# Hybrid SSD and Conformer layer on one core: decay rows repeated by DMAs, step sizes folded into exponents, sums by matmuls, more convolution taps off VectorE, three units at the start

## The chip, the core and the metric

The kernel runs on one core of a Trainium2 chip. Its engines are TensorE (PE, with its weight loads as PEld), VectorE (DVE), ScalarE (ACT), GpSimd (POOL) and SyncE (SP), which here only issues DMAs. The metric is the time of one execution on the device in microseconds (us), as the median of several runs. Profiles come from one profiled execution each.

## The reference, cut to what matters

One layer of a diffusion backbone is applied to 512 latent tokens and 128 context tokens, with a width of 1024, all in float32. The change touches the first of its two sub-layers, token mixing:

```python
h = rms_norm(x, g_pre) * (1 + sc1) + sh1
proj = h @ w_in                       # z, x/B/C of the SSD, dt, and a, g of the Conformer branch
# (A) SSD, both directions, 16 heads, chunks of 128
dt = softplus(dt_raw + dt_bias);  a_cum = cumsum(dt * a)      # per chunk and head
decay[i, j] = exp(a_cum[i] - a_cum[j])  for i >= j, else 0
y_diag[i] = sum_j (C_i . B_j) * decay[i, j] * x[j] * dt[j]
y_off[i]  = (C_i . state before the chunk) * exp(a_cum[i])
y_ssd = rms_norm((y_fwd + y_bwd + x * d_skip) * silu(z))
# (B) Conformer branch
u = a * sigmoid(g);  u = depthwise conv over 31 taps(u);  u = silu(layer_norm(u))
x = x + g1 * rms_norm(concat(y_ssd, u) @ w_out)
```

The second sub-layer is a gated FFN of width 2816 with a 3x3 depthwise convolution between its up-projection and its gate. The final SSD states of the context tokens are outputs too.

## The kernel before

Data lie with channels on the 128 partitions and the 640 tokens (512 latent, then 128 context) along the free axis. A *unit* is one weight block, 128 x 1024 f32 (512 KB), giving 128 output channels. To keep float32 accuracy in the faster float32r matmuls, each weight and each activation is split in two parts: ACT copies it to float32r (`hi`, L165 for weights, L253 for activations), and POOL or DVE subtracts (`lo`, L167, L255). `mm3` (L261) forms hi x hi, hi x lo and lo x hi for each of 8 blocks of the contraction, in two column halves (384 and 256): 48 matmuls (L268) per unit. `fetch` (L133) loads units in order on SP's queue into two raw buffers (`wr`); there are three buffers each for `hi` and `lo`, and `get_unit` asks for two units ahead.

The framework orders each engine's instructions itself, by priority and an estimate of times when the program is built; each engine then runs its own list in order. `tc.issue_after(x)` puts an instruction behind `x` on its engine; `conv31` has a negative `high_priority`, so its taps fill what is left.

The stages up to the output projection:

- *Start.* x is loaded, its norm computed (column sums L326, square root L340, spread L334), and x multiplied by it (chunks 0 to 3 on DVE, L373; 4 to 7 on POOL, L375). In four steps `ada_first` (L290) produces the modulation of two chunks, DVE applies it (L385), and the first two units, g0 and a0, multiply those chunks.
- *`dtprep`* (L448). Small DVE and ACT operations give the step sizes `DT`, the cumulative decays `ACM`, the weights `WD` and `CDs`; the decays, split in two parts, are transposed into `acHL`.
- *Pairs of heads*, p = 0 to 7, in the order of the list `seq` (L181 to 211). Each pair projects xs, z, and g, a of a later pair. `ssd(p)` (L592): POOL makes x * dt (`xd`, L600); one-column selectors multiply `acHL` so that a head's decay row appears on all partitions in PSUM (L631); ACT takes Relu(ACM - row) per chunk (L637), then Exp (L645); DVE and POOL multiply by the masked products of C and B (L648); L666 multiplies with `xd`. `decays()` (L605) does the same for exp(a_cum), with a selector cast on DVE (L608) and matmuls L612. `ssd_tokens(p + 1)` transposes x and weights it (L559), `ssd_states(p + 1)` forms the chunk states (L573, L575), copies them (L577), stores the context states and runs the recurrence on POOL (L585, L588). The states enter by L655. `ssd_tail(p)` (L678) adds, multiplies by silu(z) and squares.
- *`conv31(p)`* (L707). 31 taps: the first on ACT (L718), then one DVE instruction per tap into PSUM (L721, L724, L725). `OFF[p]` taps (9 in all) go instead as ACT products (L730) and POOL additions (L734, L736). POOL adds the results to a running sum (L742).
- *LN and the "ahead" products.* `ln_stats` (L750) makes the mean and variance by column sums; `ahead_splits` (L844) splits the first five SSD outputs; `ahead_parts` (L851) multiplies them by their weights; `layer_norm` (L826) applies norm and Silu.

After that, the output projection starts at about 423 us of the profiled execution; the FFN follows and ends it.

## Time and profile before

| | |
|---|---|
| median of 3 runs | 1012.25 us (1012.11 to 1014.71) |
| profiled execution | 1010.71 us |
| its span | 1008.9 us |
| mean granted TensorE clock | 0.993 |
| data moved by DMA | 102.76 MB, mean 102 GB/s |

A profile page gives the busy time of each engine, its share of the span and its instructions; then the busy share of 40 slices, the DMA queues, the chain of waits that ended last, and groups of instructions by source line. In a group, "out<-in" names the tiles, "xN" counts, then come busy time and mean ns of one, and the idle time before them with what ended it. In the order of time each line has start, duration, engine, line, operation, tiles and count; a bracket holds the idle time before and what released it. Matmuls overlap in the pipeline, so the mean duration of one is longer than the distance between two.

### The profile page before, as it was taken

To read this page: it belongs to the slowest core of one execution; us is meant where nothing else is said; L and a number is where in the kernel's file an instruction comes from. 1 tells how busy PE (TensorE), PEld (TensorE's weight loads), DVE (VectorE), ACT (ScalarE), POOL (GpSimd) and SP (SyncE) were. 2 spreads that over 40 slices of the span, in tenths; PEclk is the share of its full clock that TensorE was granted. 3 is DMA by queue.
4 is the path that set the end of the run, shared out by engine and by line. 5 is a ranking of instruction groups with operands and counts; after the bars stand their busy time and mean duration, and the time that the engine had idled before them with its cause. 6 is when DMAs were issued, how large, how long until landed. Compare 5 with 4: busy or idle time off the path is not lost.

```text
span 1008.9 us, 18834 instructions
## 1 busy us (share of the span) xinstructions
PE 968.3 (96%) x7655; PEld 933.7 (93%) x7655; DVE 736.1 (73%) x1093; ACT 457.9 (45%) x766; POOL 588.8 (58%) x426
## 2 busy tenths in 40 slices
PE   4999999999999989999989999999999999999995
PEld 2789999999999978899979999999999999999995
DVE  3789999989999998672286798998988988400004
ACT  6244556674553856842364754233233236322211
POOL 2333877888887896443473696454454456543444
PEclk9999999999999999999999999999999999999998
DMA  9622121122212111559463422222222222222212
GB/s 345 229 80 79 53 94 63 54 74 64 74 43 66 41 50 41 167 165 391 156 206 106 147 84 64 85 70 77 85 71 76 84 70 68 79 79 74 79 37 105
DMA packets 42934, 102.76 MB, mean 102 GB/s; under 512 B 4832, under 2 KB 12768, under 8 KB 42848
## 3 DMA queue, kind: packets, MB, share of 16 engines
q1 hardware_dynamic: 42848, 101.56, 30.4%
q8 instruction: 60, 0.98, 0.4%
q14 instruction: 26, 0.21, 0.1%
HBM read 97.87 MB, written 3.67 MB: 101 GB/s over the span
## 4 chain that ended last, share of the span: by engine, by line
PE 81%; DVE 7%; ACT 5%; POOL 3%; issue 2%; DMA 2%; SPq 0%; POOLq 0%; ACTq 0%; DVEq 0%
PE ps L268 67%; PE ps L1112 3%; PE pq L268 2%; POOL wl L167 2%; PE pq L313 2%; PE pq L666 1%; DVE T L760 1%; ACT wh L165 1%; DVE ps L721 1%; PE pq L655 1%; PE pq L573 1%; DMA wr<-in_wout 1%; PE pq L294 1%; PE pq L631 1%; DMA T<-in_xT 1%
## 5 line engine op out<-in xcount | busy, mean ns | idle before, releaser
L167 POOL TENSOR_TENSOR wl<-wr,wh 128x1024 fp32r<-128x1024 f32 (+3 forms) x127 | 291.7, 2297 | 293.3 <-ACT wh L165 287.4
L268 PE MATMUL ps<-H,wh 128*128 128x384 f32 (+1 forms) x1636 | 322.1, 310 | 4.9 <-DVE M L421 2.2
L165 ACT ACTIVATE wh<-wr 128x1024 fp32r<-128x1024 f32 (+3 forms) x131 | 131.7, 1006 | 342.6 <-PE ps L268 196.8
L268 PE MATMUL ps<-T,wh 128*128 128x384 f32 (+1 forms) x1472 | 273.1, 306 | 1.9 <-ACT S L1080 1.9
L268 PEld LDWEIGHTS ps<-H,wh 128*128 128x128 f32 x1636 | 249.0, 188 | 9.1 <-issue 4.5
L1090 DVE SCALAR_TENSOR_TENSOR S<-ps,prms,S 128x441 f32<-128x441 f32 (+2 forms) x336 | 233.4, 695 | 29.7 <-ACT S L1080 19.2
L268 PEld LDWEIGHTS ps<-T,wh 128*128 128x128 f32 x1472 | 219.3, 188 | 2.3 <-ACT S L1080 2.2
L721 DVE SCALAR_TENSOR_TENSOR ps<-u,prms,ps 128x655 f32<-128x655 f32 x223 | 200.7, 900 | 9.9 <-ACT ps L718 5.4
L268 PE MATMUL ps<-H,wl 128*128 128x384 f32 (+1 forms) x818 | 194.8, 310 | 0.0
L268 PE MATMUL ps<-T,wl 128*128 128x384 f32 (+1 forms) x736 | 166.7, 306 | 0.0
L268 PEld LDWEIGHTS ps<-H,wl 128*128 128x128 f32 x818 | 128.8, 188 | 1.6 <-issue 1.2
L268 PEld LDWEIGHTS ps<-T,wl 128*128 128x128 f32 x736 | 113.0, 188 | 0.0
L341 DVE RECIPROCAL rsm<-rsm 128x160 f32<-128x160 f32 (+2 forms) x9 | 7.3, 815 | 141.5 <-ACT rsm L340 141.5
L268 PE MATMUL ps<-S,wh 128*128 128x384 f32 (+1 forms) x420 | 87.5, 312 | 1.7 <-DVE M L923 1.2
L268 PEld LDWEIGHTS ps<-S,wh 128*128 128x128 f32 x420 | 65.9, 188 | 4.3 <-issue 2.5
L268 PE MATMUL ps<-S,wl 128*128 128x384 f32 (+1 forms) x210 | 54.4, 308 | 0.3 <-POOL wl L167 0.3
L637 ACT ACTIVATE S<-pq,ACM 128x128 f32<-128x128 f32 x140 | 40.9, 372 | 18.3 <-PE pq L631 18.1
L1080 ACT ACTIVATE S<-ps,prms 128x640 f32<-128x640 f32 x42 | 36.5, 868 | 0.0
L268 PEld LDWEIGHTS ps<-S,wl 128*128 128x128 f32 x210 | 35.0, 188 | 0.5 <-POOL wl L167 0.5
L588 POOL TENSOR_TENSOR S<-S,stmp 128x128 f32<-128x128 f32 x36 | 18.6, 517 | 15.1 <-ACT S L577 11.2
L1193 POOL TENSOR_TENSOR H<-S,S 128x640 f32<-128x640 f32 x16 | 25.2, 1578 | 0.0
L648 POOL TENSOR_TENSOR S<-S,M 128x640 f32<-128x640 f32 x14 | 22.1, 1577 | 4.4 <-ACT S L645 4.4
(353 smaller groups left out, 1276.7 us busy)
## 6 DMA issues: line engine op xcount, KB each, us to landing
wr<-in_wup SPq DMA_DIRECT2D x44, 512.0 KB, 3.4
wr<-in_win SPq DMA_DIRECT2D x36, 512.0 KB, 3.5
T<-in_wada SPq DMA_DIRECT2D x49, 256.0 KB, 5.4
wr<-in_wdown SPq DMA_DIRECT2D x16, 512.0 KB, 3.4
wr<-in_wout SPq DMA_DIRECT2D x13, 512.0 KB, 3.4
H<-in_wada SPq DMA_DIRECT2D x23, 256.0 KB, 5.5
S<-in_wada SPq DMA_DIRECT2D x16, 256.0 KB, 5.9
wr<-in_wdown SPq DMA_DIRECT2D x8, 384.0 KB, 3.1
```

The costliest lines, as they stand in the source:

```text
L165: ac.activation(hi[:, :n], raw[:, :n], AF.Copy)
L167: lo_eng.tensor_tensor(lo[:, :n], raw[:, :n], hi[:, :n].bitcast(F32), SUB)
L268: last_mm[0] = te.matmul(out, w, x[:, c0:c1], start=first and i == 0, stop=last and i == 2)
L313: te.matmul(pt[32 * j:32 * j + 32, 0:P], cts[:, kc, :], w[:, j * P:(j + 1) * P], start=kc == 0, stop=kc == KD - 1, tile_position=(0, 32 * j))
L588: gp.tensor_tensor(now, now, tmp, ADD)
L637: ac.activation(r[:, c * P:(c + 1) * P], pb[:, (c - c0) * P:(c - c0 + 1) * P], AF.Relu, scale=-1.0, bias=ACM[:, c, row:row + 1])
L648: (ve if i % 2 or last else gp).tensor_tensor(r, r, cbm[g][d], MUL)
L721: ve.scalar_tensor_tensor(acc, u[:, j:j + UO], w(j), acc, MUL, ADD)
L1080: ac.activation(out, v, AF.Identity, bias=prm_col("ffn_b", i), scale=w(1, 1))
L1090: ve.scalar_tensor_tensor(ob, vl[:, r0 + a - 1:r1 + a - 1, q0 + b - 1:q1 + b - 1], w(a, b), ob, MUL, ADD)
L1112: te.matmul(pt[:, o:o + c1 - c0], w[k] if i in (1, 2) else w[:, k * P:(k + 1) * P], x[:, c0:c1], start=k == 0 and j == 0, stop=k == KD - 1 ...
L1193: gp.tensor_tensor(f_raw[q], a, b, MUL)
```

## The change

Decay rows: `dtprep` transposes `ACM` itself, stores it in a DRAM tile `acD` (32 rows, one for each head and direction, of 640), and `load_rows(p)` reads each row back onto all partitions by DMA. ACT's Relu and Exp then work in place on those tiles; the selectors and their matmuls are gone. `load_rows(p + 1)` is called after `ssd_tail(p)`, for the last pair at the statistics.

Step sizes: exp(a_i - a_j) * dt_j becomes exp of a sum with log(dt_j) in it. `AC2` is `ACM` less log(dt), shifted by `EB`, the largest log(dt) of a row, which is added back as the bias of Exp; so `xd` is not needed and L666 takes x itself.

Sums: `ln_stats` takes the column sums of all eight results instead of POOL's running sum. Taps: `OFF` grows from 9 to 30. Start: B0 is the third unit of the first loop; parameters come in two loads, `wdts` and `ids` later; DVE does all eight multiplications of x; the Sqrt table is loaded after the first Silu. A few orders on queues are fixed by `issue_after`.

```diff
-    sy.dma_start(prms, prm)
-    ids = sb.tile([P, 32], F32, tag="idhl", name="ids")
-    sy.dma_start(ids, idhl_d)
-    wdts = sb.tile([P, KD, 32], F32, tag="DTW", name="wdts")
-    sy.dma_start(wdts, wdt)
+    NEAR = _COLS["g_mix_pre"][1]
+    sy.dma_start(prms[:, 0:NEAR], prm[:, 0:NEAR])
...
-    FIRST = ("g0", "a0")
+    FIRST = ("g0", "a0", "B0")
...
-    s_proj("B0", "C0")
+    s_proj("C0")
...
-    ac.activation(cts, cts, AF.Silu)
-
-    ac.activation(sb.tile([P, 1], F32, tag="warm", name="warm"), epsc, AF.Sqrt)
+    cond = ac.activation(cts, cts, AF.Silu)
+
+    with tc.issue_after(cond.ins):
+        ac.activation(sb.tile([P, 1], F32, tag="warm", name="warm"), epsc, AF.Sqrt)
...
-    for s in range(1, 4):
+    firsts = [(get_unit(unit_of[n][0]), psum((0, 2)[i])) for i, n in enumerate(FIRST[:2])]
+    wdts = sb.tile([P, KD, 32], F32, tag="DTW", name="wdts")
+    sy.dma_start(wdts, wdt)
+    load_ada(1)
+    sy.dma_start(prms[:, NEAR:], prm[:, NEAR:])
+    ids = sb.tile([P, 32], F32, tag="idhl", name="ids")
+    sy.dma_start(ids, idhl_d)
+    for s in range(2, 4):
         load_ada(s)
     ada_first(0)
-    rs0 = slot("S12")
-    ac.activation(rs0, prs[:, 192:192 + T], AF.Copy)
     for k in range(KD):
-        if k < 4:
-            ve.tensor_tensor(xs_[k], xs_[k], prs[:, 192:192 + T], MUL)
-        else:
-            gp.tensor_tensor(xs_[k], xs_[k], rs0, MUL)
+        ve.tensor_tensor(xs_[k], xs_[k], prs[:, 192:192 + T], MUL)
+    firsts.append((get_unit(unit_of[FIRST[2]][0]), psum(1)))
...
-        ac.activation(aexp, prm_col("a_log", 0, 32), AF.Exp)
+        with tc.issue_after(hi_ins[0].ins):
+            ac.activation(aexp, prm_col("a_log", 0, 32), AF.Exp)
...
+        ve.tensor_scalar(by(a), DT, 1e-37, None, MAX)
+        ac.activation(n, a, AF.Ln)
+        ac.activation(w, n, AF.Exp, scale=-1.0)
+        ve.tensor_tensor(w, w, a, MUL)
+        ve.scalar_tensor_tensor(n, w, -1.0, n, ADD, ADD)
+        EB = sb.tile([P, 32], F32, tag="EB", name="EB")
+        ve.tensor_tensor(EB, by(n)[:, 0, :], by(n)[:, 1, :], MAX)
+        for c in range(2, NCH):
+            ve.tensor_tensor(EB, EB, by(n)[:, c, :], MAX)
+        AC2 = sb.tile([P, NCH, 32], F32, tag="AC2", name="AC2")
+        ve.tensor_tensor(AC2, ACM, by(n), SUB)
+        ve.tensor_tensor(AC2, AC2, EB.unsqueeze(1).to_broadcast([P, NCH, 32]), ADD)
...
+        acD = dr.tile([32, T], F32, tag="acD", name="acD")
+        sy.dma_start(acD, acT[0:32, :])
+
+    rows = {}
+
+    def load_rows(p):
+
+        last = p == NPAIR - 1
+        for h in range(2):
+            for d in range(2):
+                row = 2 * p + h + 16 * d
+                r = rows[p, h, d] = slot(f"{'H' if last else 'S'}{(12 if last else 6) + 2 * h + d}")
+                sy.dma_start(r, acD[row:row + 1, :].to_broadcast([P, T]))
+        for d in range(2):
+            e = rows[p, d] = slot(f"S{10 + d}")
+            for h in range(2):
+                row = 2 * p + h + 16 * d
+                sy.dma_start(e[64 * h:64 * h + 64, 0:L], acD[row:row + 1, 0:L].to_broadcast([64, L]))
...
-            ac.activation(t[:, 0:4 * P], pt, AF.Copy)
+            state_out[0] = ac.activation(t[:, 0:4 * P], pt, AF.Copy)
...
-        xd = []
-        for d in range(2):
-            o = slot(("M4", "H11")[d] if last else f"S{2 + d}")
-            a = 16 * d + 2 * p
-            gp.tensor_tensor(hq(o), hq(xt), DT[:, :, a:a + 2].unsqueeze(3).to_broadcast([P, NCH, 2, 64]), MUL)
-            xd.append(o)
...
             for d in range(2):
-                pea = psq(d)
-                te.matmul(pea[:, 0:L], sel[:, d].rearrange("p h q -> p (h q)"), acHL[:, 0:L], start=True, stop=True)
-                ea.append(slot(f"S{10 + d}"))
-                peas.append(pea)
-            for o, pea in zip(ea, peas):
-                ac.activation(o[:, 0:L], pea[:, 0:L], AF.Exp)
+                o = rows.pop((p, d))
+                ac.activation(o[:, 0:L], o[:, 0:L], AF.Exp)
+                ea.append(o)
...
+                r = rows.pop((p, h, d))
+                for c in range(NCH):
+                    rc = r[:, c * P:(c + 1) * P]
+                    if last and d:
+                        with tc.issue_after(z_done[0].ins):
+                            ve.tensor_scalar(rc, rc, AC2[:, c, row:row + 1], 0.0, SUB, MIN)
+                        continue
+                    ac.activation(rc, rc, AF.Relu, scale=-1.0, bias=AC2[:, c, row:row + 1])
...
-            ssd_exp[0] = ac.activation(r, r, AF.Exp, scale=1.0 if last and d else -1.0)
+            ssd_exp[0] = ac.activation(r, r, AF.Exp, scale=1.0 if last and d else -1.0,
+                                        bias=EB[:, 16 * d + 2 * p + h:16 * d + 2 * p + h + 1])
...
-                                  xd[d][:, c * P + 64 * h:c * P + 64 * h + 64],
+                                  xt[:, c * P + 64 * h:c * P + 64 * h + 64],
...
-    OFF = [1, 2, 1, 2, 1, 2, 0, 0]
+    OFF = [6, 6, 4, 4, 4, 4, 2, 0]
...
-        if p == 0:
-            usum[0] = slot("S17")
-            gp.tensor_copy(usum[0], o)
-        elif p < NPAIR - 1:
-            gp.tensor_tensor(usum[0], usum[0], o, ADD)
...
-        colsum(pm, 0, usum[0], 0, 160, True, False)
-        colsum(pm, 0, uc[NPAIR - 1], 0, 160, False, True)
+        for p in range(NPAIR):
+            colsum(pm, 0, uc[p], 0, 160, p == 0, p == NPAIR - 1)
...
+    bT[0] = slot("M2")
+    conv3_silu(firsts[2][1], 8, bT[0])
     dtprep()
...
             ssd_tail(it[1])
+            if it[1] + 2 < NPAIR:
+                load_rows(it[1] + 1)
         elif it[0] == "stats":
+            load_rows(NPAIR - 1)
...
             hi, lo = slot(f"H{k}", F32R), slot(LOSLOT[k], F32R)
-            ac.activation(hi, tp[k], AF.Copy)
+            with tc.issue_after(state_out[0].ins):
+                ac.activation(hi, tp[k], AF.Copy)
```

## The prediction

> **What bounds the kernel now.** I read the page first (shares, chain), then cut the span into windows by stage, then the groups, and last the order of time where a term of the sum stands. The page:

> ```profile
> span 1008.9 us, 18834 instructions
> PE 968.3 (96%) x7655; PEld 933.7 (93%) x7655; DVE 736.1 (73%) x1093; ACT 457.9 (45%) x766; POOL 588.8 (58%) x426
> PE 81%; DVE 7%; ACT 5%; POOL 3%; issue 2%; DMA 2%; SPq 0%; POOLq 0%; ACTq 0%; DVEq 0%
> ```

> PE is busy 96% of the span and 81% of the chain that ended last; DVE's 73% is an average over a mixing half in which it is full and an FFN half in which it is not. The windows (time, then busy and count of PE, PEld, DVE, ACT, POOL, granted clock, DMA share, GB/s) say where:

> ```profile
> 28.60:55.70 27.10, 26.26 (x315) 21.82 (x314) 16.86 (x33) 8.56 (x16) 6.49 (x5) 0.98 0.49 180
> 55.70:72.00 16.30, 14.05 (x99) 13.83 (x98) 16.23 (x24) 4.90 (x9) 6.74 (x3) 1.00 0.30 99
> 72.00:250.00 178.00, 178.00 (x1325) 176.40 (x1326) 169.17 (x225) 101.19 (x194) 134.04 (x115) 1.00 0.22 68
> 250.00:300.00 50.00, 47.18 (x352) 45.62 (x351) 46.30 (x59) 28.36 (x61) 40.10 (x33) 1.00 0.18 59
> 300.00:349.70 49.70, 49.70 (x375) 49.20 (x375) 47.38 (x63) 29.39 (x61) 37.52 (x32) 1.00 0.17 54
> 349.70:423.30 73.60, 67.57 (x580) 59.48 (x579) 61.30 (x74) 50.78 (x93) 53.45 (x48) 1.00 0.21 67
> ```

> From 72 to 250 us PE has no gap at all, and DVE is busy 95%: two engines are full, and PE is the tighter one. After 423 us come the output projection and the FFN, which the diff does not touch; I leave them as they are. So only 423 us can change, in three places: PE work that goes, PE gaps that close, and the start.

> **The change, part by part.** (1) *Decay rows by DMA.* The row-selecting matmuls L631 and L612 go. A busy mean overstates a pipelined matmul, so I price them by the distance of starts:

> ```profile
> 157.48 0.34 PE L631 MATMUL pq<-HL,idr 128*128 128x384 f32 x1
> 157.65 0.28 PE L268 MATMUL ps<-H,wl 128*128 128x256 f32 x1
> 158.63 0.28 PE L631 MATMUL pq<-HL,idr 128*128 128x256 f32 x1
> 158.74 0.74 PE L268 MATMUL ps<-H,wh 128*128 128x384 f32 x4
> 180.40 0.39 PE L612 MATMUL pq<-HL,sel 128*128 128x512 f32 x1
> 180.63 0.28 PE L268 MATMUL ps<-H,wh 128*128 128x256 f32 x1
> ...
> L631 PE MATMUL pq<-HL,idr 128*128 128x384 f32 (+1 forms) x56 | 17.2, 312 | 0.5 <-ACT S L637 0.5
> L631 PE MATMUL ps<-HL,idr 128*128 128x384 f32 (+1 forms) x8 | 3.1, 384 | 0.7 <-ACT H L637 0.7
> L612 PE MATMUL pq<-HL,sel 128*128 128x512 f32 x16 | 5.3, 395 | 0.0
> ```

> That is 0.17 + 0.11 us for a pair of L631 and 0.23 for an L612: 32 x 0.28 + 16 x 0.23 = 12.6 us of PE, all in stages where PE is full or nearly. In their place each pair gets eight DMAs: four of 320 KB and four of 128 KB, 1.8 MB, on SP's queue with the weights. The trace has no read that repeats one row. The nearest is x itself, same tile (128 x 640 f32), same queue; the dearest SP wait on compute stands beside it:

> ```profile
> T<-in_xT SPq DMA_DIRECT2D x8, 320.0 KB, 5.8
> SPq L578 <- ACT S L577: 29.5, 9, 8.8
> ```

> 5.8 us was measured at the saturated start; in the mixing stage (68 GB/s, DMA share 0.22) there is room: 1.8 MB per pair of about 42 us adds 43 GB/s. The rows for pair p+1 must land between L666 of pair p and the Relu of pair p+1, most of a period, so I cost them at nothing; below nothing they cannot be, and from above they cost what a late weight costs (a rival). The Relu now reads SBUF instead of PSUM; no Relu of that kind is in the trace, but 20 of them a pair, 0.1 us dearer or cheaper, are 2 us on an engine that is busy 101 of 178 us: hidden.

> (2) *Step sizes folded into the exponent.* The 16 POOL multiplies of L600 go, for ten or so small DVE operations and two table switches in the preparation, beside five projections that need none of it. (3) *Sums by matmuls.* POOL's L742 goes; the LN statistics get six more column sums. (4) *Taps.* 30 instead of 9 taps go to ACT and POOL.

> ```profile
> L721 DVE SCALAR_TENSOR_TENSOR ps<-u,prms,ps 128x655 f32<-128x655 f32 x223 | 200.7, 900 | 9.9 <-ACT ps L718 5.4
> L608 DVE CAST sel<-ids 128x256 fp32r<-128x256 f32 x8 | 11.4, 1424 | 0.3 <-PE pq L612 0.3
> L730 ACT ACTIVATE T<-u,prms 128x512 f32<-128x512 f32 (+1 forms) x18 | 9.2, 560 | 2.2 <-DVE u L705 1.4 <-POOL T L736 0.7
> L736 POOL TENSOR_TENSOR T<-T,T 128x640 f32<-128x640 f32 x6 | 9.5, 1582 | 5.2 <-DVE T L725 5.2
> L742 POOL TENSOR_TENSOR S<-S,T 128x640 f32<-128x640 f32 x6 | 10.3, 1718 | 0.2
> L600 POOL TENSOR_TENSOR S<-S,DT 128x640 f32<-128x640 f32 x8 | 10.6, 1341 | 1.2 <-PE pq L666 1.2
> 387.45 0.46 PE L326 MATMUL ps<-M,ones 128*32 128x160 f32 x8
> 387.84 0.94 PE L573 MATMUL pq<-S,M 128*128 128x128 f32 x6
> ```

> DVE: 21 x 0.90 + 11.4 (the casts of L608) = 30 us less; the four windows from 55.7 to 349.7 us hold 279 us of DVE work. ACT: 21 x 2 x 0.56 = 24 more. POOL: 21 x 1.58 = 33 more, against 16 x 1.34 + 6 x 1.72 = 32 less (the last two L600 run longer, so a little more): even. PE: 6 x 0.39 = 2.3 us more for the column sums, to a stage with gaps. DVE falls by a tenth where PE falls by a thirtieth, so PE stays the bound of the mixing stage and DVE stops being the close second; that is why I count nothing for DVE between 72 and 250 us. A tap is dearer where it goes (1.1 on ACT and 1.6 on POOL for 0.9 on DVE). [...] The trace speaks for the move, by ACT's 101 us of 178.

> (5) *The start.* B0 joins g0 and a0, so three units fill PE while the chunks of x come; half of the parameters load later; all eight x multiplies are on DVE; the Sqrt table is loaded ahead.

> ```profile
> 12.38 1.28 ACT L340 ACT_TABLE_LOAD   x1
> 18.63 6.10 POOL L375 TENSOR_TENSOR T<-T,S 128x640 f32<-128x640 f32 x4 [17.39 <-ACT S L370]
> 20.65 1.06 ACT L165 ACTIVATE wh<-wr 128x1024 fp32r<-128x1024 f32 x1 [0.40 <-DMA wr<-in_win]
> 25.63 1.03 PE L360 MATMUL pq<-T,wdts 128*32 128x512 f32 x1 [4.99 <-issue]
> 26.53 5.26 POOL L167 TENSOR_TENSOR wl<-wr,wh 128x1024 fp32r<-128x1024 f32 x2
> 71.94 0.84 PE L268 MATMUL ps<-H,wh 128*128 128x384 f32 x4 [2.25 <-DVE M L421]
> ```

> The 1.28 us load stands on the path to the first norm and goes. POOL's first weight remainder starts at 26.53 because POOL multiplies x until 24.7; freed, it can follow the split at 20.65 + 1.06, some 4.8 us sooner. PE idles 4.99 us before 25.63, and closes part of it. Between 28.6 and 55.7 PE has nearly no gap (26.26 of 27.1), so interleaving B0 does not by itself add much; it takes the 2.25 us wait at 71.94 away, since B0's convolution is then queued ahead of the preparation. I take 6 us for the earlier start (between 0, if DMA at share 0.97 of its time sets it anyway, and 8) and 2 for the wait.

> (6) *The tail.* In 349.7 to 423.3 PE shows 73.6 - 67.57 = 6.0 us of gaps, and gaps under 0.3 us are hidden in modelled ends; in 250 to 300 another 2.8. DVE held the last convolution back; with 30 us less it ends earlier, and the normalisation after it. The rows of the last pairs no longer wait for a PSUM bank, PE and ACT in turn. I take 4 us (between -2, where the new sums fall in no gap, and 9), and nothing for 250 to 300, where POOL's order made the gap and POOL is no freer.

> **Sum:** -12.6 + 2.3 - 6 - 2 - 4 = -22.3 us. On the profiled execution, 1010.7 us (span 1008.9), that gives 988.4; the median shown, 1012.25, lies 1.5 above it, so 990.

> **Rivals.** *A: POOL's or ACT's order eats half the gain.* The weight remainders (L167) share POOL with 21 more adds, of which the first two pairs get nine. In 250 to 300 us POOL's order already cost PE 2.8 us; such a gap in each of the six pairs with many taps brings 17 us back, 1007, in half of them 998. Or the tail is turned round: the diff lets ACT copy the five early outputs (L847), from which the "ahead" products are made, only after the state copy (L577) of the last pair. Before, it was the other way:

> ```profile
> 344.02 1.39 ACT L847 ACTIVATE H<-T 128x640 fp32r<-128x640 f32 x2
> 392.67 1.06 ACT L577 ACTIVATE S<-pq 128x512 f32<-128x512 f32 x2
> 166.93 4.01 PE ps L268 x28
> ```

> The ahead products are 8 x 30 matmuls at 4.01 / 28 = 0.143 us, 34 us. If that state copy stayed where it is, they would run from about 396 to 430 + some 4 us of the last pair, 11 us later than the 423 of now, against 18 us won ahead of them: -7, 1003. Against both: POOL's total is even, and its adds can wait until the LN statistics; the last state copy was late because its transposes stood behind the L631 of the pair before, which are gone.

> *B: SP's queue (slower).* SP issues in order. The rows of pair p+1 go into tiles that PE's L666 and POOL's L682 of pair p still read, so their issue waits for these, and behind it wait the weights, for which PE waits.

> ```profile
> wr<-in_win SPq DMA_DIRECT2D x36, 512.0 KB, 3.5
> SPq L141 <- POOL wl L167: 711.3, 116, 11.9
> ```

> PE's stock is two units of 48 matmuls, 13.8 us; landing 3.5, split 1.06 and remainder 2.6 (5.26 / 2) take 7.2 of it, so a block of up to 6.6 us is covered. Each us beyond costs PE a us, in seven pairs. At the 8.8 us of the longest L578 wait that is 15 us, 1005. It decides from 6.6 + 22.3 / 7 = 9.8 us; at 12 us, as the longest wait of L141, it is 38 us, 1028. For: eight more DMAs per pair with two kinds of wait ahead of the weights. Against: SP mostly sits waiting for a weight buffer anyway (711 us in total), and the rows can be issued in such a wait. A read of one repeated row that is slow at its source would act in the same way: it has to take 35 of the 42 us of a pair, 52 GB/s, before weights starve, and the kernel moves 68 GB/s there without effort.

> *C: all gaps close.* With 8 us at the start, 9 in the tail and the 2.8 of 250 to 300: -12.6 + 2.3 - 8 - 2 - 9 - 2.8 = -32 us, 980; with the hidden gaps somewhat lower, 975.

> That the change does nothing at all could only be if DVE stayed the bound of the mixing stage, and DVE loses 30 us, more than PE.

> **How the numbers follow.** Forecast 990, its own range 983 to 998: 0.56. A, 998 to 1008: 0.19. C, 974 to 983: 0.14. B, 1005 to 1030: 0.08. Slower by something not seen here: 0.03. The likeliest case gives 990. For 8 in 10 the range takes in C and most of A: 975 to 1006. About 0.3%, 3 us, is what a measurement of this kernel can tell from no change. Faster by more than that (under 1009): 0.56 + 0.19 + 0.14 = 0.89, less a part of A's upper end, plus the low end of B: 0.88. Within 0.3%: 0.04. Slower: 0.08.

> **What would show it.** (1): no PE matmul on decay rows, and PE without gaps from 72 to 300 us, with starts of successive L268 still 0.143 apart; the interval between two pairs' L666 falls by 1.5 us. A gap in front of L268 released by ACT's split with SP waiting on a row load is B; one released by POOL's L167 behind an add is A. (4): DVE's busy share in 72 to 250 us falls from 95% to below 90%; were it still 95%, DVE would be the bound and point (4) wrong. (5): the first L268 comes before 28.64, at 23 to 25 us, and the three units are through by about 55. (6): the first product of the output projection, at 423 now, comes at about 401, and L577 of the last pair before L847. The FFN after it keeps its length; if the end moves by more or less than that first product, something behind it has changed that I took as fixed. The forecast is wrong in its sum if the start wins nothing (DMA sets it) or the tail keeps its 6 us.

## The result, and the profile after

The changed kernel is slower: 1028.59 us (median of four runs, 1024.61 to 1030.59) against 1012.58 before (four runs), a ratio of 1.0149 with a 95% interval of 1.0115 to 1.0183. Its profiled execution took 1030.59 us, the slowest of its four, and that of before 1010.71, faster than all of its four, so that the account below has 19.9 us between the two spans to explain, where the medians differ by 16.0. The page of the changed kernel (span, busy times, chain of waits by engine):

```profile
span 1028.8 us, 18846 instructions
PE 977.2 (95%) x7623; PEld 942.2 (92%) x7623; DVE 700.5 (68%) x1073; ACT 475.5 (46%) x806; POOL 580.5 (56%) x419
PE 72%; DVE 10%; ACT 9%; DMA 5%; issue 2%; POOL 2%; SPq 0%; POOLq 0%; ACTq 0%; DVEq 0%
```

DVE lost 36 us of work, as meant, and the row selection is gone. PE's share of the chain fell from 81% to 72%, and what came in its place is DVE, ACT and, new, DMA. The same windows as before (PE, PEld, DVE, ACT, POOL, granted clock, DMA share, GB/s), the last one up to the first matmuls of L313, which stand in the output projection and moved from 448.4 to 460.0 us:

```profile
28.60:55.70 27.10, 26.27 (x275) 22.09 (x272) 13.71 (x32) 7.53 (x12) 4.33 (x5) 0.92 0.53 193
...
72.00:250.00 178.00, 168.94 (x1238) 165.53 (x1237) 153.07 (x213) 116.01 (x234) 137.63 (x117) 0.99 0.35 105
...
300.00:349.70 49.70, 47.95 (x385) 46.70 (x384) 44.72 (x58) 24.26 (x50) 40.77 (x43) 1.00 0.37 111
349.70:460.00 110.30, 100.94 (x787) 94.71 (x785) 77.25 (x101) 66.20 (x114) 53.10 (x38) 0.92 0.35 114
```

From 72 to 250 us PE now stands still for 9 of 178 us, where it had no gap; and the granted clock is below 1 in three of the four rows. The longest waits of PE from 60 to 460 us (us in total, times, longest), before and after; the changed kernel has its own line numbers (L424 was L421, L604 was L577, L664 was L655, the Relu of the rows L646 was L637, and the Y product, which multiplies the decay products with x, is L666 before and L675 after):

```profile
PE pq L666 <- DVE S L657: 2.4, 1, 2.4
PE ps L268 <- DVE M L421: 2.2, 1, 2.2
PE pq L573 <- ACT S L616: 1.8, 2, 1.6
```

```profile
PE ps L268 <- DVE S L424: 4.4, 5, 2.0
PE ps L268 <- ACT wh L164: 3.7, 1, 3.7
PE pq L664 <- ACT S L604: 3.4, 2, 2.7
PE pq L600 <- POOL S L586: 2.8, 1, 2.8
PE ps L268 <- DVE S L752: 2.2, 2, 1.5
PE ps L268 <- DVE T L752: 1.8, 1, 1.8
```

No single wait took the place of another: PE waits for three engines, in a dozen places, never more than 4 us. Three things add up to the difference, and each shows in a view of its own.

**Stalls.** I add up how far the starts of successive matmuls lie apart beyond 0.30 us (0.60 at half clock), from 50 to 460 us: 11.8 us before, 22.7 after.

```profile
358.40 0.98 PE L666 MATMUL pq<-S,S 128*64 128x128 f32 x14 [2.37 <-DVE S L657]
```

```profile
186.48 0.80 PE L664 MATMUL pq<-M,st 128*128 128x128 f32 x2 [2.73 <-ACT S L604]
```

and the windows of the grid in which they fall (PE busy first, granted clock third from the end), before and then after:

```profile
353.98:357.40 3.42, 2.05 (x18) 1.85 (x17) 3.42 (x4) 2.56 (x7) 3.34 (x4) 1.00 0.15 44
357.40:360.81 3.41, 2.41 (x35) 2.24 (x36) 3.41 (x6) 0.06 (x1) 2.62 (x5) 1.00 0.37 129
```

```profile
179.59:183.00 3.41, 3.41 (x29) 3.41 (x28) 3.34 (x5) 3.41 (x7) 1.53 (x2) 1.00 0.00 0
183.00:186.41 3.41, 0.75 (x6) 0.49 (x4) 3.16 (x6) 3.41 (x7) 3.41 (x3) 1.00 0.21 58
186.41:189.82 3.41, 3.34 (x15) 3.34 (x16) 3.26 (x5) 3.39 (x5) 3.41 (x3) 0.50 0.39 139
```

Before, the border of two windows splits the gap, PE is idle for 1.4 us in one and 1.0 in the other, and the clock stays. After, one window is idle for 2.66 us, and PE gets half its clock in the whole of the next: 15 matmuls, against 29 in the first window shown. Between 55 and 700 us the kernel before has no such window, the changed one has 23.9 us of them.

**Spacing.** In the up projection of the FFN nothing was changed and PE has no gap. Still 200 us of it, before and after:

```profile
600.00:800.00 200.00, 200.00 (x1446) 199.60 (x1445) 179.56 (x294) 63.22 (x76) 100.98 (x51) 1.00 0.24 77
```

```profile
600.00:800.00 200.00, 200.00 (x1416) 199.59 (x1415) 176.30 (x289) 66.37 (x81) 105.79 (x57) 1.00 0.23 75
```

1416 matmuls instead of 1446, 2.1% fewer, at a full granted clock: the start behind a 384-column matmul comes about 176 ns after it instead of 168.6.

### The profile page after: what moved, and what is told of

Same layout as the page of the kernel before. It is cut to its first block, busy times and chain, and to the rows that moved or that the text cites. A ratio compares the mean times of both kernels' runs of the same rounds, so it can differ in the third digit from the quotient of the medians.

```text
span 1028.8 us, 18846 instructions
## 1 busy us (share of the span) xinstructions
PE 977.2 (95%) x7623; PEld 942.2 (92%) x7623; DVE 700.5 (68%) x1073; ACT 475.5 (46%) x806; POOL 580.5 (56%) x419
## 4 chain that ended last, share of the span: by engine, by line
PE 72%; DVE 10%; ACT 9%; DMA 5%; issue 2%; POOL 2%; SPq 0%; POOLq 0%; ACTq 0%; DVEq 0%
PE ps L268 60%; DMA S<-acD 3%; DVE ps L730 3%; PE ps L1123 3%; ACT S L646 2%; PE pq L268 2%; PE pq L313 2%; ACT wh L164 1%; PE pq L664 1%; PE pq L675 1%; ACT S L653 1%; PE pq L600 1%; POOL wl L166 1%; PE pq L294 1%; DVE M L1021 1%
## 5 line engine op out<-in xcount | busy, mean ns | idle before, releaser
L268 PE MATMUL ps<-H,wh 128*128 128x384 f32 (+1 forms) x1636 | 326.6, 314 | 12.6 <-DVE S L424 4.4
L268 PE MATMUL ps<-T,wh 128*128 128x384 f32 (+1 forms) x1472 | 276.9, 309 | 1.8 <-ACT S L1091 1.8
L268 PEld LDWEIGHTS ps<-H,wh 128*128 128x128 f32 x1636 | 249.9, 189 | 21.9 <-issue 8.0
L268 PEld LDWEIGHTS ps<-T,wh 128*128 128x128 f32 x1472 | 221.0, 188 | 2.2 <-ACT S L1091 2.1
L730 DVE SCALAR_TENSOR_TENSOR ps<-u,prms,ps 128x655 f32<-128x655 f32 x202 | 181.7, 900 | 18.8 <-ACT ps L727 15.3
L268 PE MATMUL ps<-H,wl 128*128 128x256 f32 (+1 forms) x818 | 192.6, 310 | 0.0
L268 PE MATMUL ps<-T,wl 128*128 128x384 f32 (+1 forms) x736 | 168.9, 309 | 0.0
L268 PEld LDWEIGHTS ps<-H,wl 128*128 128x128 f32 x818 | 127.8, 188 | 1.0 <-issue 1.0
L268 PEld LDWEIGHTS ps<-T,wl 128*128 128x128 f32 x736 | 112.8, 188 | 0.0
L268 PE MATMUL ps<-S,wh 128*128 128x384 f32 (+1 forms) x420 | 89.5, 318 | 4.7 <-ACT wh L164 3.7
L268 PEld LDWEIGHTS ps<-S,wh 128*128 128x128 f32 x420 | 67.7, 192 | 6.9 <-ACT wh L164 3.9
L268 PE MATMUL ps<-S,wl 128*128 128x384 f32 (+1 forms) x210 | 55.1, 313 | 0.3 <-POOL wl L166 0.3
L646 ACT ACTIVATE S<-S,AC 128x128 f32<-128x128 f32 x140 | 43.1, 389 | 9.2 <-DMA S<-acD 9.2
L743 POOL TENSOR_TENSOR T<-T,T 128x640 f32<-128x640 f32 x23 | 36.1, 1570 | 10.1 <-ACT T L739 8.9
L739 ACT ACTIVATE T<-u,prms 128x512 f32<-128x512 f32 (+1 forms) x60 | 30.4, 552 | 12.7 <-POOL T L743 11.0
L268 PEld LDWEIGHTS ps<-S,wl 128*128 128x128 f32 x210 | 35.5, 191 | 0.5 <-POOL wl L166 0.5
## 6 DMA issues: line engine op xcount, KB each, us to landing
wr<-in_wup SPq DMA_DIRECT2D x44, 512.0 KB, 3.5
wr<-in_win SPq DMA_DIRECT2D x36, 512.0 KB, 3.6
wr<-in_wdown SPq DMA_DIRECT2D x16, 512.0 KB, 3.5
wr<-in_wout SPq DMA_DIRECT2D x13, 512.0 KB, 3.5
```

The source lines that it names most:

```text
L268: last_mm[0] = te.matmul(out, w, x[:, c0:c1], start=first and i == 0, stop=last and i == 2)
L646: ac.activation(rc, rc, AF.Relu, scale=-1.0, bias=AC2[:, c, row:row + 1])
L730: ve.scalar_tensor_tensor(acc, u[:, j:j + UO], w(j), acc, MUL, ADD)
L739: ac.activation(t[:, b:c], u[:, a:a + c - b], AF.Copy, scale=w(j))
L743: gp.tensor_tensor(far, far, t, ADD)
```

## The experiments

Times are medians, each beside the kernel before on the same chip (1011.7 to 1014.2); stalls and half clock are counted as above, in each profiled execution. The texts of what was expected give names to theories of the loss: ADDRESS (where the tiles lie), LOOP (waits for the row loads), START (the third unit holds up the preparation), TAPS, ROWS (the loads cost more than they save), SINGLE PART (one part is to blame), ORDER (each engine's list is laid anew, and worse) and WORK (what is added or taken away decides, not the order).

**Place of the tiles.** Removing the tiles `DT`, `ACM` and `idr` (1408 bytes of each partition) and adding `EB` and `AC2` (768) moved all that is allocated behind them. The weight tiles `wr`, `wh` and `wl` lie 640 bytes lower, which on a grid of 512 bytes is 384 further. e1 puts every tile back:

```diff
+    ids = sb.tile([P, 32], F32, tag="idhl", name="ids")      # at its old place
+    wdts = sb.tile([P, KD, 32], F32, tag="DTW", name="wdts")
...
+    slot("S12")                                             # first use where it was
...
+        EB = sb.tile([P, 32], F32, tag="EB", name="EB")     # in the place of idr
+        AC2 = sb.tile([P, NCH, 32], F32, tag="AC2", name="AC2")
```

> The changed kernel with every SBUF tile put back at the address that it had before the change (the tiles that the change removed stay reserved); every engine gets the same instructions in the same order. Theory ADDRESS (the matmuls of L268 are spaced by where their tiles lie): the 384-column starts go from 175-176 ns back to 168-171, the up projection of the FFN from 269.7 back to 264 us, the whole 8 to 10 us faster, about 1019. Theories LOOP, START and TAPS (the time went into waits between the engines): no difference beyond 3 us.

1023.26 us, 5.3 less than the changed kernel where ADDRESS had said 8 to 10, and 1447 matmuls in 600 to 800 us. Then the weight tiles alone (e5), and the kernel before with its weight tiles moved up by 384 bytes, to the changed kernel's place on that grid (e6):

```diff
         gs = gains_of['pre'] = sb.tile([P, KD, 2], F32, tag="gs2", name="gs2")
+        sb.tile([P, 160], F32, tag="pad", name="pad")       # e5; 96 instead of 160 in e6
```

> The changed kernel with 640 bytes left free ahead of the weight tiles wr, wh and wl, so that these alone lie where they lay before the change; all other tiles stay as the change has them, and so do all instructions. If the spacing of L268 hangs on the place of the weights, the up projection's 384-column starts fall from 176.0 to 168.4 ns as in e1_addresses and the time by 5 us, to about 1023.5. If it hangs on the place of the x tiles or on other tiles, the spacing stays at 176 and the time at 1028.

> The kernel before with 384 bytes left free ahead of the weight tiles: they then lie at the same remainder to 512 bytes as in the changed kernel (384), all instructions as before. If that remainder sets the spacing, the up projection's 384-column starts rise from 168.6 to 176 ns, its stage from 264 to 270 us, and the time by 5 to 7 us, to about 1019. If only the exact place counts, or the spacing has another cause, it stays at 1013.

e5 took 1021.75 us (ratio to before 1.0091, interval 1.0058 to 1.0124), e6 1021.89 (1.0087, 1.0065 to 1.0109). The same window of e5 and of e6:

```profile
600.00:800.00 200.00, 200.00 (x1447) 199.60 (x1446) 180.78 (x296) 66.12 (x78) 107.24 (x56) 1.00 0.24 77
```

```profile
600.00:800.00 200.00, 200.00 (x1416) 199.59 (x1415) 176.15 (x288) 62.42 (x74) 100.94 (x52) 1.00 0.24 75
```

The spacing goes with the place of the weight tiles, in both directions, with every instruction the same. It is worth 6.8 us in the changed kernel (1028.59 to 1021.75) and 9.0 in the kernel before (1012.87 to 1021.89). The place of the weights is shown as the cause of this part, at 5 to 9 us; 9 us of loss are left, and with what was forecast some 30.

**The row loads.** They land late:

```profile
S<-acD SPq DMA_DIRECT2D x28, 320.0 KB, 5.2
S<-acD SPq DMA_DIRECT2D x32, 128.0 KB, 5.3
```

and ACT, whose 806 instructions stand in the trace in the order of its list, waits for them (60 to 460 us of the changed kernel):

```profile
ACT S L629 <- DMA S<-acD: 28.4, 5, 9.6
...
ACT S L646 <- DMA S<-acD: 9.2, 6, 2.3
```

That is 37.6 us, and by theory LOOP the source of the stalls. e2 loads three of a pair's four rows a pair ahead, e7 two of them and both tiles of the state decay:

```diff
+            if p + 1 < NPAIR:
+                load_early(p + 1)        # odd pairs into S2, S3, S17 (e7: and a new tile X0); e2: for p + 2 < NPAIR
             ssd(p)
```

> The changed kernel with three of the four decay rows of a pair loaded a pair ahead, into tiles that nothing reads then (S2, S3, S17 for the odd pairs). Theory LOOP (the row loads stand between the Y product of one pair and the Relus of the next, 4 to 7 us in each of seven pairs): PE's stalls between 72 and 460 us fall from 23.7 us to 12-15 and the time by 8 to 12 us, to about 1018. Theory ADDRESS or START: no difference beyond 3 us, since the pairs then only wait for something else.

> The changed kernel with rows for two pairs held at once: both tiles of the state decay and two of the four row tiles of a pair are loaded a pair ahead, the other two behind the Y product of the pair before as in the change (they are read 10 Relus later). Theory LOOP: the waits of ACT for rows (37.6 us in the changed kernel between 60 and 460 us, 25.6 with three row tiles early) fall below 10, DVE's and PE's idle time with them, and the time falls by 5 to 10 us, to about 1020. Rival ORDER (each engine runs a list laid down beforehand, and another wait takes the place of this one): ACT's waits for rows go and the time stays within 3 us.

1026.53 and 1024.55 us, stalls 21.6 and 25.2. But neither took the waits away: e2 leaves 25.6 us of them, and in e7 ACT waits 38 us, as in the changed kernel:

```profile
ACT S L641 <- DMA S<-acD: 19.9, 3, 10.1
ACT S L658 <- DMA S<-acD: 18.2, 6, 8.6
```

The early loads had been put ahead of the pressing ones on SP. So these two decide nothing. e13 puts them behind:

```diff
+            ssd(p)
+            if p + 1 < NPAIR:
+                with tc.issue_after(row_ins[0].ins):    # the last pressing row load
+                    load_early(p + 1)
```

> The changed kernel with rows for two pairs held at once as in e7, but the loads that are not pressing (the next pair's) issued behind the pressing ones (the two row tiles of the pair at hand); in e7 they stood ahead of these, and ACT waited for rows as long as before (38 us). Weight tiles at a place with short spacing (168 ns in e7). Theory LOOP: ACT's waits for rows fall below 12 us, PE's stalls between 50 and 460 us from 23-27 to below 16, the time to 1008-1016. Theory ORDER: ACT's waits for rows fall, PE stalls elsewhere for as long, the time stays at 1018-1025.

```profile
ACT S L660 <- DMA S<-acD: 21.5, 7, 7.0
```

ACT's waits for rows fall to 21.5 us, not below 12 as LOOP had it; the stalls stay at 22.4, and the time is 1020.76 us, against 1021.75 of e5, which has the short spacing too. The same kernel measured once more (e15) shows how far two measurements differ:

> The kernel of e13 once more, in the same shift of the chip: it measures what two runs of one program differ by here. Both theories: within 3 us of e13.

1021.90 us. Forty per cent of the waits went and the time did not move. e18 (below) is this kernel with another order, and has still fewer:

```profile
ACT S L660 <- DMA S<-acD: 10.0, 7, 3.0
```

With 10.0 us of waits left of 37.6, its stalls are 23.8 us and its time 1020.16: the stalls do not follow ACT's waits for rows, and LOOP falls. That the loads cost nothing does not follow (see the stalls by stage, below). What the loads save shows in e8, the changed kernel with selectors and matmuls again:

> The changed kernel with the decay rows made by matmuls again (row selection, PSUM banks and the casts of sel as before the change); the step sizes stay in the exponents, the taps, the column sums and the three units at first stay as changed. Theory ROWS (the row loads cost more, by ACT standing before them, than the 12.6 us of matmuls that they save): the time falls by 10 to 20 us, to 1008-1018, in spite of 12.6 us more of PE and 10 us more of DVE. Rival (the loss is in the other parts: the start, the step sizes, the taps): the time rises by 5 to 12 us, to 1034-1040.

1046.78 us, 18 more: ROWS was wrong, the loads pay in the changed kernel, and by more than the rival's 5 to 12 us. Its span is 24.0 us above that of e5 (spacing is short in both: e8 has 1436 matmuls in the 198.1 us in which PE is busy from 600 to 800 us): stalls 3.0 more (29.7), half of the half-clock time 10.2 more (37.5 against 17.1), and 10.8 us are left for the matmuls that came back, which the forecast put at 12.6.

**Other parts taken back.** e3 starts with two units, e4 has the old taps:

```diff
-    FIRST = ("g0", "a0", "B0")
+    FIRST = ("g0", "a0")                                    # e3
...
-    OFF = [6, 6, 4, 4, 4, 4, 2, 0]
+    OFF = [1, 2, 1, 2, 1, 2, 0, 0]                          # e4
```

> The changed kernel with two units in flight at first, as before the change; B0 is a projection of its own again. Theory START (B0 among the firsts keeps PE from the dt product, so that the preparation starts at 67.5 instead of 54.6 us and the first pair's Y product comes at 163.9 instead of 151.7): the first Y comes back to 152-154 us and the time falls by 6 to 12 us. Theory LOOP: the first Y comes sooner, but the pairs behind it wait for rows as before, and the time stays within 3 us, or is 2 us worse by the wait for B0's convolution.

> The changed kernel with 9 taps on ACT and POOL as before the change instead of 30. Theory TAPS (POOL and ACT got too much, and the weight remainders stand behind the adds): POOL's longest waits of SP for weight buffers shrink and the time falls by 5 to 10 us. Theories LOOP and ADDRESS: DVE has 19 us more to do and is full again, and the time is the same or up to 6 us longer.

1035.31 and 1046.27 us. In e3 the preparation does begin at 51.7 us and the first Y product comes at 144.0, as START had it, but the next ones come at 182 and 231, the stalls rise to 32.0, and the time by 7: START falls. e4 says the same of the taps: 18 us worse without them, so TAPS falls too. No theory had foreseen the size of either loss.

**Each part alone.** If taking a part back costs 7 to 18 us, each should win alone. The kernel before with one part, all tiles at their places:

> The kernel before with one part of the change alone: 30 taps on ACT and POOL instead of 9; all tiles stay at their addresses. Theory ORDER (each engine's list, laid down beforehand, fitted well in the kernel before, and each part of the change lays it anew with stalls of PE that eat the gain): PE, which had no stall from 72 to 250 us, gets some there, and the time is 0 to 10 us longer. Rival SINGLE PART (one part of the change is to blame, and it is not this one, since taking it back in e4 made the changed kernel 18 us slower): 5 to 15 us faster, about 1003.

> The kernel before with one part alone: the decay rows loaded by DMAs, the step sizes still multiplied on POOL, all tiles that are left at their addresses. Theory ORDER: PE saves 12.6 us of row selection, ACT then stands before the loads, and stalls of PE give back most of it: within 6 us of before, 1007 to 1019. Rival SINGLE PART (the rows are not to blame, as e8 says): about 12 us faster, 1000. Rival LOOP alone: slower by what ACT waits, 10 to 20 us.

> The kernel before with one part alone: the sums of the conv outputs by matmuls instead of POOL's running sum, all tiles at their addresses. By the forecast's term: 2.3 us of PE more, or hidden, 10 us less on POOL: within 3 us. Theory ORDER: the lists are laid anew by this small edit too, and it moves the time by up to 10 us.

> The kernel before with one part alone: the start (three units in flight, parameters and tables loaded later, all x multiplies on DVE), all tiles at their addresses. By the forecast's term: 6 to 8 us faster. Theory START: the preparation begins 13 us later, the first pair's Y 12 us later, and the time is 5 to 12 us longer. Theory ORDER: either, with stalls of PE behind 72 us.

Taps 1033.95 (its profiled run 1023.67), rows 1050.53, sums 1017.49, start 1030.74 us: all slower, by 22, 39, 6 and 19 us, three of them by more than the whole change. ORDER had said up to 10 us for the taps and at most 6 for the rows, LOOP 10 to 20 for the rows, SINGLE PART a gain: none of them foresaw 22 and 39. In the start's case PE is ahead at first (counted in columns, by 5.8 us at 150 us and 2.9 at 240) and falls back behind 250 us, where no instruction was changed:

```profile
350.00:460.00 110.00, 97.13 (x758) 87.45 (x757) 84.82 (x103) 68.48 (x119) 67.95 (x56) 0.92 0.26 83
```

PE is busy 97 of 110 us at a clock of 0.92, where before (quoted below) it was 104 at 1.00. Parts that lose alone and lose when taken back are not a sum of costs. What all these kernels share is that the framework laid each engine's list anew; that this is why they lose is so far an argument.

**The tail's order.** e14 drops the two orders that the change lays down there (the other is that of the last pair's differences behind z):

```diff
-            with tc.issue_after(state_out[0].ins):
-                ac.activation(hi, tp[k], AF.Copy)
+            ac.activation(hi, tp[k], AF.Copy)
```

> The changed kernel with the weight tiles at their old place (as e5, 1021.75) and without two orders that the change lays down: the copies of the five early outputs need not come after the last state copies, and the last pair's differences not after z. Rival A of the forecast (the tail turned round): the stalls between 350 and 450 us, 11.7 us in e5, fall to 6-8, and the time by 4 to 8 us, to about 1016. Theory ORDER: the tail is laid anew, and the time stays within 4 us of 1022 or rises.

1026.61 us, 5 more than e5; the stalls from 350 to 450 us rise from 11.7 to 18.4. The order was a help: the prediction's rival A falls. What A feared is there to see (the early copies start at 373 us, behind the last state copy, instead of at 344), but with them at 359 us in e14 the output projection's first product with the late half comes at 431.8 us, and in e5 at 431.9.

**The order alone.** e16 is the kernel before with one number changed, the priority of the conv sums when the lists are laid. Work, tiles and addresses are the same.

```diff
-        with tc.high_priority(offset=-3000):
+        with tc.high_priority(offset=-300):
```

> The kernel before with every instruction, tile and address as it was, but with the conv sums given a priority of -300 instead of -3000 when the order is laid; so only the order on the engines differs. Theory ORDER: the order before was an unusually good one; another with the same work gives PE stalls in 72 to 450 us and half-clock windows behind them, and the time is 5 to 25 us longer. Rival WORK (the parts of the change cost by what they add in work or loads): the time stays within 3 us of before.

1022.00 us, ratio 1.0089 (1.0063 to 1.0115). The window from 350 to 460 us, before and in e16:

```profile
350.00:460.00 110.00, 103.86 (x954) 93.89 (x957) 87.58 (x106) 70.19 (x119) 69.11 (x57) 1.00 0.36 118
```

```profile
350.00:460.00 110.00, 98.15 (x832) 90.71 (x831) 80.95 (x100) 67.13 (x114) 74.81 (x56) 0.97 0.28 88
```

PE's waits in e16 are of the same kind as those of the changed kernel, small and in new places:

```profile
PE ps L268 <- ACT wh L165: 4.3, 1, 4.3
PE ps L631 <- DVE H L634: 2.6, 1, 2.6
PE pq L573 <- POOL S L559: 2.3, 1, 2.3
```

So an order can cost 8 us with no work added: that much of ORDER is shown, for one other order of the kernel before. In the changed kernel another order was tried twice, in e5 (priority 0) and in e13 (priority -300):

> The changed kernel with the weight tiles at their old place (e5, 1021.75) and the conv sums at priority 0 instead of -3000 when the order is laid; work, tiles and addresses as in e5. Theory ORDER: the time moves by 5 us or more, up or down, with PE's stalls between 50 and 460 us. Rival WORK: within 3 us of e5.

> The kernel of e13 and e15 (1020.8 and 1021.9) with the conv sums at priority -300; work, tiles and addresses as there. Theory ORDER: the time moves by 5 us or more, up or down, with PE's stalls; if down, this could come below the kernel before. Rival WORK: within 3 us of e13.

1030.31 us, 8.6 more than e5, as ORDER had it; and 1020.16, no different from e13, as WORK had it. Neither these nor any other kernel of the study came below the kernel before.

**The stalls by stage.** The new order of e16 opens no gap from 72 to 250 us, the row loads alone (e10) do; e16 first:

```profile
72.00:250.00 178.00, 178.00 (x1317) 176.39 (x1316) 165.68 (x223) 100.19 (x193) 134.22 (x115) 0.99 0.22 68
```

```profile
72.00:250.00 178.00, 165.86 (x1195) 163.62 (x1195) 147.45 (x199) 103.57 (x206) 127.73 (x113) 0.96 0.34 101
```

PE is busy there for 176.4 to 178.0 us in every kernel that keeps the rows on matmuls and is otherwise that of before (e6, e9, e11, e12, e16 and before itself), for 161.8 to 169.2 in all 13 profiles with row loads, and for 172.7 in e8, the changed kernel without them. So the gaps of this stage come for the larger part with the row loads, in each order tried; by which path is open, since e18 has them (169.2) with few waits for rows. Behind it a new list is enough: from 350 to 460 us PE is busy for 103.9 us in the kernel before and in e6, which has its list, and for 89.2 to 102.6 in all the others, with row loads and without.

**The account.** For the profiled executions, in us; "half" is the time at half clock from 55 to 700 us, of which about one half is lost:

| kernel | span | stalls | half | matmuls, 600 to 800 us |
|---|---|---|---|---|
| before | 1008.9 | 11.8 | 0 | 1446 |
| changed | 1028.8 | 22.7 | 23.9 | 1416 |
| e5, weights at their old place | 1020.0 | 26.7 | 17.1 | 1447 |
| e6, before with weights moved | 1019.9 | 11.7 | 6.8 | 1416 |
| e12, start alone | 1025.8 | 22.5 | 27.3 | 1446 |
| e10, rows alone | 1050.6 | 39.4 | 54.6 | 1416 |
| e16, before in another order | 1020.8 | 19.0 | 13.7 | 1447 |

(e10 has its weights at their old place; a half-clock window behind 600 us takes matmuls from its last column.) Changed minus before: stalls +10.9, half clock 23.9 / 2 = +12.0, the place of the weights +7.6 (e6's 11.0 less 6.8 / 2 for its half clock), PE work -12.6 + 2.3 = -10.3; together +20.2, measured +19.9. e10: +27.6 + 27.3 - 12.6 = 42.3, measured 41.7. e16: 7.2 + 6.9 = 14.1, measured 11.9; for the other kernels such sums come out between 3 us too low (e18) and 9 too high (e14), part of a half-clock window being idle anyway (2.9 of the changed kernel's 23.9 us), so that the agreement of the first two is in part luck. What made the stalls is not told by this account.

## Why the prediction was wrong

It said 990 us with a range of 975 to 1006; the time is 1028.6. By its steps:

- **(1) PE work.** The 12.6 us of row selection did go: e10's account and e8's 11 us bear the term out. What failed is the step from there to the time: "PE stays the bound of the mixing stage", with what leaves PE counted in full and nothing for new gaps. "PE without gaps from 72 to 300 us" was named as the sign, and 9 us of gaps from 72 to 250 refute it. Where the sum had 22.3 us of gain, the runs show 10.3 us less of PE work against 10.9 us of new stalls, 12.0 lost at half clock and 7.6 by the place of the weights.
- **(1) The row loads at nothing.** This term failed. Put alone into the kernel before (e10), the loads open 12 us of gaps between 72 and 250 us, where another order opens none, and cost 39 us in all, where 12.6 were to be won. They are not hidden from ACT either (37.6 us of waits); but the waits are not the path, since with 10.0 us of them (e18) the stalls are as long. Whether the loads do it by the lists that are laid around them or in another way is open.
- **(2), (3) Step sizes and sums.** The sums alone cost 6 us, of which 2.3 were forecast; that kernel (e11) also has 10.2 us at half clock. The step sizes were not tried alone.
- **(4) Taps.** DVE's share from 72 to 250 us fell to 153 of 178, 86%, as foretold. "I count nothing for DVE" did not hold: with the taps put back the changed kernel is 18 us slower, with the taps alone the kernel before is 22 slower (its profiled execution was 10 us faster than the other four, so that no trace shows the whole loss). The price of a tap, 0.90 us on DVE and 1.6 on POOL in both kernels, did not decide it; that the order of the lists did is argued, not shown.
- **(5) The start.** Half right. POOL did begin its first remainder 5 us sooner (21.53 us), but the eight products on DVE, until 23.4 us, now stand ahead of the modulation, which DVE applies at 26.25 us; before it did so at 24.98. The changed kernel's start, in order of time:

```profile
17.45 5.93 DVE L377 TENSOR_TENSOR T<-T,ps 128x640 f32<-128x640 f32 x8 [2.59 <-PE ps L334]
...
21.53 4.67 POOL L166 TENSOR_TENSOR wl<-wr,wh 128x1024 fp32r<-128x1024 f32 x2 [20.28 <-ACT wh L164]
...
23.95 2.27 DVE L384 TENSOR_TENSOR asc<-asc,prms 128x4 f32<-128x4 f32 x1
26.25 1.52 DVE L388 TENSOR_SCALAR T<-T,asc,modv 128x512 f32<-128x512 f32 x4
...
29.41 1.44 PE L268 MATMUL ps<-H,wh 128*128 128x384 f32 x4
```

  The first L268 starts at 29.41 instead of 28.64, not at 23 to 25. With the start alone (e12) PE leads by up to 5.8 us, close to the forecast 6, and the later stages then lose it.
- **(6) The tail.** Forecast to close its gaps by 4 us. The pairs do end sooner, the last Y product starts at 394.3 instead of 416.1 us; but the first product of the output projection with the late half, forecast at about 401 us, comes at 433.4 instead of 423.3, behind a wait of 3.7 us for its weights, and two of the half-clock episodes (17.1 us) begin there.
- **The FFN** "keeps its length": it does not, by the place of the weights, 5.7 us in the up projection (264.0 to 269.7). Of this the forecast had no trace.
- **Rivals.** The slow side was held open by one mechanism, SP's queue (B). It was another: PE waited for a late weight once in this stage, 3.7 us, and that weight was late because ACT had worked without a pause since 417 us, not because of SP. A fell with e14, C with the gaps.

## What to carry to other kernels

Where an engine is full because its list fits, what is taken off it is not yet won: count gaps from a new layout of the lists as a term of its own (here, for the same work in another order, 8 us more in two trials and nothing in the third), and compare a change with several orders of the kernel before. Try each part alone, and look at the stage where the busiest engine had no gap: the part that opens one there (here the row loads) is not free, even if no wait names it. Look for stalls of 2 us and more on TensorE: here each could bring a window of 3.41 us at half clock (in the counts below all 73 windows with 2.0 us and more idle did), and so, by an estimate of 2.0 us and half of 3.41, cost nearly twice its length. When tiles come or go, keep the others where they lie, or check a stage that was not touched for the spacing of its matmuls (here 176 ns for 168.6).

## What the runs showed of the hardware

**The clock.** In the 20 profiles, over all windows of the 3.41 us grid from 60 us on that ran at full clock: with less than 1.1 us of PE idle (the profile models a matmul's end), 5266 windows, none was followed by half clock; from 1.1 to 1.5 us, 5 of 68; from 1.5 to 2.0 us, 32 of 66; with 2.0 us and more, all 73. So less than six tenths of a window idle was enough, whole or in pieces (in the changed kernel's window before 541.40 us 1.58 us were idle, no gap being longer than 0.99). The grid is read from the traces: in the changed kernel the shortest piece at half clock lasts 3.41 us (186.41 to 189.82), and those between 55 and 700 us begin at 186.41, 367.32, 432.17 and 541.40 us, 53, 19 and 32 times that length apart. The gap of 2.73 us above was enough, and by the counts the 2.37 us one, with 1.4 and 1.0 us of it in two windows, escaped by its place on the grid.

**The weights' place.** Matmuls of 384 and 256 columns with a new weight block each were spaced about 168.6 and 118.5 ns in the up projection with the weight tiles at their old place (or 256 bytes further on a grid of 512, in e7: 1447 matmuls in 600 to 800 us; e13 and e18, at the same place as e7, have 1439 and 1438), and about 176 and 117.5 ns with them 384 further (e6 and the changed kernel). Only these places were tried, 512 bytes is the author's way of counting them, and why it is so stays open; in the mixing stage, from 72 to 250 us, the mean spacing of the 384-column matmuls differed by 1.1 ns (174.5 before, 175.6 in the changed kernel).
